# One cast and one subtraction per weight block of 2048 columns, in place of two of 1024 each

## The chip, the cores and the metric

The kernel runs on one core of one Trainium2 chip. What counts is the device time of one launch, in microseconds (us), as the median of several runs. The launch reads float32 inputs from device memory and writes a float32 output.

## What is computed

The reference is a two-layer trunk over 256 tokens of width 1024. Each layer is a half-step feed-forward block (FFN), a mixer (differential attention beside an mLSTM), and a second FFN, each between two RMS norms:

```python
def _swiglu(h, w_in, w_out):
    gate, up = jnp.split(h @ w_in, 2, axis=-1)          # w_in: 1024 x 5632
    return (jax.nn.silu(gate) * up) @ w_out             # w_out: 2816 x 1024

for l in range(DEPTH):                                   # DEPTH = 2
    g = norm_gains[l]
    h = _swiglu(_rmsnorm(x, g[0]), ffn_w_in[l, 0], ffn_w_out[l, 0])
    x = x + 0.5 * _rmsnorm(h, g[1])
    h = _mixer(_rmsnorm(x, g[2]), mix_w_in[l], mix_w_out[l], ...)
    x = x + _rmsnorm(h, g[3])
    h = _swiglu(_rmsnorm(x, g[4]), ffn_w_in[l, 1], ffn_w_out[l, 1])
    x = x + 0.5 * _rmsnorm(h, g[5])
```

Almost all of the arithmetic is the products with the weights, which are read once, in 164 blocks of 1 MB of float32.

## The kernel before

**Weights.** The weights come as *pieces* of 128 x 2048 float32 (1 MB), 33 to an FFN and 16 to a mixer. `fetch` (L283) loads a piece into a tile `wr`, or for every fourth piece of an FFN into a tile `wx`; there are three of the one and one of the other. A product in full precision is made of three matmuls on rounded operands, so every piece is taken apart into a rounded high part and a low part. `halved` (L291) does this for 1024 columns: ScalarE (ACT) casts them to the high tile `wh` (L295) and VectorE (DVE) subtracts that from the raw piece into the low tile `wl` (L296). A piece takes two such pairs of instructions. TensorE (PE) then does high x high, high x low and low x high (L506 to L508 in `mm3`; L762 in the pair steps; L737 and L742 at the end of an FFN).

**Buffers of the parts.** Seven tiles `wl` and seven tiles `wh` of 1024 columns rotate; three of every ten halves go to a third pool, `k4` (six of 1024 columns), which the mixer also uses for its own tiles through `t4`.

**An FFN.** The hidden units are taken in 11 chunks of 256. `STEPS` says what is loaded and done when: `I` are the two input pieces of a chunk, `L` an output piece, `O` the output matmuls of a chunk (`out_part`), `P` a *pair* of chunks whose first product is done with seven block products in place of eight. `pair_blocks` (L310) makes these seven operands: four raw pieces and the sums of some of them, which DVE adds in halves of 1024 columns (L322) into the tiles `qk` and `wt`, cast and subtracted like the pieces. The activations of a chunk go ACT, DVE, then through `planes` (an ACT copy), a transposing DMA and `hT` (another ACT copy) to the operands `hh` (ACT, L676) and `hl` (DVE, L677) of the output matmuls.

**The end of an FFN.** After the second pair step (`P8`) the last chunk is computed transposed by `in_turned` (L729), into four banks: two named `pin`, two named `ptr`. `ffn_block` (L689) evacuates each of these (ACT copies `su<-pin`, `su<-ptr`, L695; DVE L696 and L697). Directly behind `in_turned` on PE come the output matmuls of the pair's first chunk, whose operand is `hh<-hT` (L676); they are L506 to L508 on the banks `bk`. Meanwhile ACT has to do, for the pair: a SiLU `u<-u`, the copy `planes<-h`, and after its DMA `hT<-h` and `hh<-hT`; the same once more for the pair's second tokens (`planes<-v`, `hT<-v`).

**What sets the order.** A scheduler with its own estimate of times orders the instructions on each engine and decides what stands ahead of what; PE's order is written out only at the very end and the very start of an FFN or mixer (`manual_schedule`). Each engine then works through its own list strictly in order: an instruction that has to wait holds up all that stands behind it. The DMA lists on SyncE (SP) work in the same way.

**Exceptions.** In an FFN that follows a mixer or FFN, the first pieces' casts are tied to the norm before (`self.turns`), and are left in halves by the change as well; so are the mixer's pieces.

Of the kernel before, what the change touches and what calls it, by code (L numbers as in the profile page):

```python
# [17 lines left out]
F32 = mybir.dt.float32  # L18
F32R = mybir.dt.float32r
U16 = mybir.dt.uint16  # L20
AF = mybir.ActivationFunctionType
ALU = mybir.AluOpType
AX = mybir.AxisListType
PSUM = bass.MemoryType.PSUM

P = 128
D = 1024
S = 256
NT = S // P
# [106 lines left out]
class _Trunk:  # L136
    def __init__(self, tc, a, out, pools):
        self.tc, self.nc, self.a, self.out = tc, tc.nc, a, out
        self.const, self.wr, self.wl, self.wh, self.tr, self.k2, self.k4, self.ded, self.hp, self.sm, self.ps = pools
        self.piece_at = 0  # L140
        self.parts = None
        self.raws, self.four = 0, False
        self.n = 0
        self.turns = []
        self.halves = 0
        self.both = [None, None]
        self.lend = True

# [11 lines left out]
        return self.k2.tile(list(shape), dt, tag=tag, bufs=bufs, name=self.name(nm))  # L160

    def t4(self, nm, shape):
        return self.k4.tile(list(shape), F32, tag="k4", name=self.name(nm))

    def small(self, nm, shape, bufs=None):
        return self.sm.tile(list(shape), F32, tag=nm, name=self.name(nm))
# [105 lines left out]
    def piece(self):  # L272


        parts = self.begin_piece()
        return [parts(), parts()]

# [13 lines left out]
    def halved(self, raw):  # L291
# [8 lines left out]
            self.after(iv, [ov] if ov else [])  # L300
        return hi, lo

    def spare(self):
        if self.parts is None:
            self.qk = self.ded.tile([P, 4, S], F32, name="qk")
            self.wt = self.ded.tile([P, NT, 2, 2, P], F32, name="wt")
            self.parts = [self.qk.rearrange("p b s -> p (b s)"), self.wt.rearrange("p t a b j -> p (t a b j)")]
        return self.parts

    def pair_blocks(self):  # L310


        def fetch():
            raw = self.fetch()
            return [raw[:, j] for j in range(2)]

        def split(raw):
            return [self.halved(raw[j]) for j in range(2)]

        def add(out, a, b):  # L320
            for j in range(2):
                self.nc.vector.tensor_tensor(out[j], a[j], b[j], op=ALU.add)  # L322

        b11, b12 = fetch(), fetch()
        w = {"P1": split(b11)}
        run = self.spare()
        add(run, b11, b12)
        w["P5"] = split(run)
        b22 = fetch()
        add(run, run, b22)  # L330
        w["P6"] = split(run)
        add(b12, b12, b22)
        w["P7"] = split(b12)
        b21 = fetch()
        w["P2"] = split(b21)
        w["P3"] = split(b22)
        add(run, run, b21)
        w["P4"] = split(run)
        return w

    def pair_tokens(self, both, kept):
# [28 lines left out]
        def split(i):  # L370
            hi, lo = (tiles[i // 2][:, :, n + i % 2, :] for n in (0, NT))
            self.ffn_hilo(s, hi, lo)
            return hi, lo
# [9 lines left out]
        apart((0, 0), (0, 1))  # L383
        yield x1, x2, split(2), x4

    def half_tiles(self):

        pools = (self.k4, "k4", self.k4, "k4") if self.lend and self.halves % 10 in (2, 5, 8) else (self.wl, "wl", self.wh, "wh")
        self.halves += 1
        return [pools[n].tile([P, 1024], F32R, tag=pools[n + 1], name=self.name(nm)) for n, nm in ((0, "wl"), (2, "wh"))]  # L390

    def raw_tile(self, i):
        self.raws += 1
# [103 lines left out]
    @staticmethod  # L497
    def cols(piece, k):

        c = slice((k % 2) * 512, (k % 2) * 512 + 512)  # L500
        hi, lo = piece[k // 2]
        return hi[:, c], lo[:, c]
# [419 lines left out]

    def mixer(self, pre, gi_post):
        self.mixer_buffers()
        m = _Mixer(self, pre, gi_post // 3)
        ws = [self.piece(), self.piece()]
        self.lend = False
        ws1 = [self.piece()]
        pins, pins1 = [self.bank_pin()], [self.bank_pin()]
        m.part(0, 0, pins[0], ws[0])  # L930
        m.part(0, 1, pins[0], ws[1])
        m.gate_part(0)
        m.conv_input(0, pins[0])
        yield "second"
        m.part(0, 0, pins1[0], ws1[0])
        m.conv_input_t(0)
        pins.append(self.bank_pin())
        ws1.append(self.piece())
        m.gate_part(1)
        gpost = []  # L940
        m.traverse(self, pins[1], ws, pins1, ws1, lambda: gpost.append(self.load_gpost(gi_post)))
        gpost = gpost[0]


        self.lend = True
        ws = [self.piece() for _ in range(4)]
        po = [[self.bank_bk() for _ in range(2)] for _ in range(NT)]

        def outp(t, part, hf):
            for k in range(4):  # L950
                yh, yl = m.yT[t][part]
                self.mm3(po[t][hf], yh[:, k, :], yl[:, k, :], *self.cols(ws[2 * part + k // 2], 2 * (k % 2) + hf),
                         start=part == 0 and k == 0, stop=part == 1 and k == 3)

        outp(0, 0, 0)
        m.outputs_ml(0)
        outp(0, 0, 1)
        outp(0, 1, 0)
        m.outputs_ml(1)
        outp(0, 1, 1)  # L960
        yield "done", po[0], gpost
        outp(1, 0, 0)
        outp(1, 0, 1)
        yield "next"
        outp(1, 1, 0)
        outp(1, 1, 1)
        yield "done", po[1], gpost
# [472 lines left out]
def _trunk(tc, a, out, phases=3 * L):  # L1440
    nc = tc.nc
    with contextlib.ExitStack() as st:
        def pool(name, bufs, **kw):
            return st.enter_context(tc.tile_pool(name=name, bufs=bufs, **kw))

        fill = pool("fill", 1)
        fill.tile([P, FILL // 4], F32, name="fill")
        wr, wl, wh, trp, k4 = pool("wr", 3), pool("wl", 7), pool("wh", 7), pool("tr", 4), pool("k4", 6)
        hp, k2, const, ded = pool("hp", 4), pool("k2", 10), pool("const", 1), pool("ded", 1)
        const.tile([P, CFILL // 4], F32, name="cfill")  # L1450
        pools = (const, wr, wl, wh, trp, k2, k4, ded, hp, pool("sm", 2), pool("ps", 1, space=PSUM))
        tr = _Trunk(tc, a, out, pools)
        tr.x = [tr.const.tile([P, D], F32, name=f"x{t}") for t in range(NT)]
        tr.early = {}
        tr.start()
        tr.users = []
        tr.table("silu_and_others")
        tr.half = tr.const.tile([P, 16], F32, name="c_half")
        nc.gpsimd.memset(tr.half, -0.5)
        tr.run(phases)  # L1460
# [17 lines left out]
```

## Time and profile before

| | |
|---|---|
| median of 3 runs | 940.39 us (940.22 to 941.68) |
| the profiled execution | 940.3 us, span 938.5 us, granted TensorE clock 0.998 |
| PE busy | 931.4 us, 99% of the span, 4427 matmuls |
| DVE busy | 775.5 us, 83%, 1079 instructions |
| ACT busy | 668.4 us, 71%, 1033 instructions |
| DMA | 189.34 MB, 202 GB/s on average |

A row of a group reads: line, engine, operation, output<-inputs, partitions x elements, count, then total busy us and mean ns of one, then the idle time of the engine just before these instructions and what ended it. A row of a timeline reads: start in us from the start of the span, duration in us of the whole row (with x2, of both), engine, line, operation, and in brackets idle time before it and what released it. Rows that overlap by a tenth of a microsecond are normal: an engine starts the next instruction before the last one's end is written.

Where the work lies: FFN 1 of layer 0 runs from the start to about 175 us, the first mixer to about 300, then two FFNs to about 640, the second mixer to about 765, and the last FFN to the end. The ends of the four FFNs' `in_turned` are at 166, 453, 629 and 916 us.

### The profile page before, as it was taken

Reading aid. Unit: us, or ns where it says so; the run is one execution under the profiler, and the core shown is the slowest. Engines: PE = TensorE matmul, PEld = TensorE weight load, DVE = VectorE, ACT = ScalarE, POOL = GpSimd, SP = SyncE. Lnnn points to the kernel's source line nnn. Section 1 sums busy time; section 2 is a strip of 40 time slices with the busy share of each in tenths; the row PEclk is TensorE's granted clock in tenths of the full one; section 3 lists DMA queues with packets and bytes.
Section 4 is the critical chain, followed back from the end, with each engine's and each line's share of the span. In section 5 each row is a group of like instructions: output and inputs, shape, how many; then the busy total and the mean of one; then the engine's idle time right before and its main releaser. Section 6 shows DMA issues by size and latency. Waiting matters only on the chain.

```text
span 938.5 us, 12082 instructions
## 1 busy us (share of the span) xinstructions
PE 931.4 (99%) x4427; PEld 771.5 (82%) x4427; DVE 775.5 (83%) x1079; ACT 668.4 (71%) x1033; POOL 29.4 (3%) x57
## 2 busy tenths in 40 slices
PE   9999999999999999999999999999999999999997
PEld 7888888888888888888888888888888888888885
DVE  7989797889867899788698987968898588986974
ACT  8967786677856868676587865866778478766862
POOL 2000000000020000000000000000001100000000
PEclk9999999999999999999999999999999999999999
DMA  9957857346362866838468585473554348486531
GB/s 354 342 169 275 251 192 218 119 152 221 138 232 90 303 167 225 303 107 309 121 237 257 172 267 189 155 237 135 189 193 169 146 157 302 148 300 184 186 115 46
DMA packets 69882, 189.34 MB, mean 202 GB/s; under 512 B 45274, under 2 KB 46426, under 8 KB 49086
## 3 DMA queue, kind: packets, MB, share of 16 engines
q1 hardware_dynamic: 69246, 187.95, 59.1%
q8 instruction: 35, 0.57, 0.2%
q10 hardware_dynamic: 576, 0.61, 0.2%
q14 instruction: 25, 0.20, 0.1%
HBM read 177.01 MB, written 1.05 MB: 190 GB/s over the span
## 4 chain that ended last, share of the span: by engine, by line
PE 99%; DVE 0%; ACT 0%; POOLq 0%; DVEq 0%; issue 0%; ACTq 0%
PE pin L506 11%; PE pin L508 10%; PE pin L507 10%; PE bk L506 10%; PE bk L507 10%; PE bk L508 10%; PE ptr L762 9%; PE pin L762 7%; PE ptr L507 3%; PE ptr L506 3%; PE ptr L508 3%; PE ptr L737 2%; PE pin L737 2%; PE ptr L532 1%; PE ptr L1100 1%; PE pin L742 1%
## 5 line engine op out<-in xcount | busy, mean ns | idle before, releaser
L296 DVE TENSOR_TENSOR wl<-wr,wh 128x1024 fp32r<-128x1024 f32 x262 | 313.6, 1221 | 42.2 <-ACT wh L295 39.4
L295 ACT ACTIVATE wh<-wr 128x1024 fp32r<-128x1024 f32 x262 | 269.5, 1055 | 55.9 <-PE bk L508 15.8
L506 PE MATMUL pin<-wh,both 128*128 128x512 f32 x432 | 171.3, 399 | 0.0
L507 PE MATMUL pin<-wl,both 128*128 128x512 f32 x432 | 168.4, 390 | 0.0
L508 PE MATMUL pin<-wh,both 128*128 128x512 f32 x432 | 168.2, 390 | 0.0
L507 PE MATMUL bk<-wl,hh 128*128 128x512 f32 x352 | 136.3, 389 | 0.0
L506 PE MATMUL bk<-wh,hh 128*128 128x512 f32 x352 | 135.8, 390 | 0.0
L508 PE MATMUL bk<-wh,hl 128*128 128x512 f32 x352 | 133.4, 389 | 0.0
L508 PEld LDWEIGHTS pin<-wh,both 128*128 128x128 f32 x432 | 81.1, 188 | 17.4
L506 PEld LDWEIGHTS pin<-wh,both 128*128 128x128 f32 x432 | 81.3, 188 | 17.2 <-issue 0.7
L507 PEld LDWEIGHTS pin<-wl,both 128*128 128x128 f32 x432 | 81.3, 188 | 15.5
L295 ACT ACTIVATE wh<-wx 128x1024 fp32r<-128x1024 f32 x62 | 64.3, 1055 | 31.9 <-PE bk L508 10.2
L762 PE MATMUL ptr<-wh,both 128*128 128x512 f32 x256 | 84.0, 389 | 0.0
L296 DVE TENSOR_TENSOR wl<-wx,wh 128x1024 fp32r<-128x1024 f32 x62 | 74.7, 1220 | 10.2 <-ACT wh L295 9.5
L508 PEld LDWEIGHTS bk<-wh,hl 128*128 128x128 f32 x352 | 66.1, 188 | 13.8
L506 PEld LDWEIGHTS bk<-wh,hh 128*128 128x128 f32 x352 | 66.1, 188 | 13.5
L507 PEld LDWEIGHTS bk<-wl,hh 128*128 128x128 f32 x352 | 66.1, 188 | 13.4
L762 PE MATMUL pin<-wh,both 128*128 128x512 f32 x192 | 63.0, 389 | 0.0
L762 PEld LDWEIGHTS ptr<-wh,both 128*128 128x128 f32 x256 | 48.0, 188 | 10.0
L507 PE MATMUL ptr<-wl,both 128*128 128x512 f32 x128 | 49.8, 389 | 0.0
L508 PE MATMUL ptr<-wh,both 128*128 128x512 f32 x128 | 49.8, 389 | 0.0
L762 PE MATMUL ptr<-wl,both 128*128 128x512 f32 x128 | 49.8, 389 | 0.0
(263 smaller groups left out, 1464.2 us busy)
## 6 DMA issues: line engine op xcount, KB each, us to landing
wr<-in_w_dram SPq DMA_DIRECT2D x131, 1024.0 KB, 5.1
wx<-in_w_dram SPq DMA_DIRECT2D x31, 1024.0 KB, 5.0
gpost<-in_gpost_dram SPq DMA_DIRECT2D x6, 512.0 KB, 6.2
wr<-in_w_dram SPq DMA_DIRECT2D x2, 512.0 KB, 6.3
wr<-in_w_dram SPq DMA_DIRECT2D x3, 256.0 KB, 4.5
x<-in_x_dram SPq DMA_DIRECT2D x3, 256.0 KB, 5.2
h<-planes SPq DMA_TRANSPOSE x32, 3.3
out_dram<-x SPq DMA_DIRECT2D x2, 256.0 KB, 2.1
```

The lines of the kernel that those rows point to most:

```text
L295: ia = nc.scalar.activation(hi, raw, AF.Copy)
L296: iv = nc.vector.tensor_tensor(lo, raw, hi.bitcast(F32), op=ALU.subtract)
L506: mm(ps, xh, wh, start=start, stop=False)
L507: mm(ps, xh, wl, start=False, stop=False)
L508: mm(ps, xl, wh, start=False, stop=stop)
L532: nc.tensor.transpose(ptr[:, k, :], x[:, (4 * hf + k) * P:(4 * hf + k + 1) * P], self.ident)
L737: self.nc.tensor.matmul(b, self.cols(w[kh], k)[0][:, c], both[kh][:, k].rearrange("p i t -> p (i t)"), start=kh == 0 and k == 0, stop=Fals ...
L742: self.nc.tensor.matmul(b[:, 0:NT * P], self.cols(w[kh], k)[1][:, c], both[kh][:, k, 0:NT].rearrange("p i t -> p (i t)"), start=False, sto ...
L762: self.nc.tensor.matmul(b, st[:, k, :], self.cols(w, k)[mv], start=new and k == n == 0, stop=k == 3 and n == 2, skip_group_check=True)
L1100: self.T(ptr[:, b, :], a[:, b * P:(b + 1) * P], self.tr.ident)
```

## The change

`whole` casts and subtracts a piece of an FFN with one ACT and one DVE instruction of 2048 columns. The tiles for the parts become one pool `w` of seven tiles of 2 x 1024 columns for high and low together, with three more in `k4`; the bytes are the same as before. `halved` stays for mixer pieces and for the first pieces of an FFN, and takes the halves of one such tile. The sums of a pair lie side by side in one tile `sums`, and each is added, cast and subtracted by one instruction of 2048 columns. By count, ACT has 135 instructions fewer, DVE 167 (135 subtractions and 32 additions); PE, SP and POOL have as many as before.

```diff
     def piece(self):
+        if self.four and not self.turns:
+            return self.whole(self.fetch())
         parts = self.begin_piece()
         return [parts(), parts()]
...
+    def whole(self, raw):
+        lo, hi = self.piece_tiles()
+        self.cut = self.nc.scalar.activation(hi, raw, AF.Copy)
+        self.nc.vector.tensor_tensor(lo, raw, hi.bitcast(F32), op=ALU.subtract)
+        return [(hi[:, j], lo[:, j]) for j in range(2)]
...
     def pair_blocks(self):
-        def fetch():
-            raw = self.fetch()
-            return [raw[:, j] for j in range(2)]
-        def split(raw):
-            return [self.halved(raw[j]) for j in range(2)]
+        fetch, split = self.fetch, self.whole
         def add(out, a, b):
-            for j in range(2):
-                self.nc.vector.tensor_tensor(out[j], a[j], b[j], op=ALU.add)
+            self.nc.vector.tensor_tensor(out, a, b, op=ALU.add)
...
+    def piece_tiles(self):
+        v = []
+        for nm in ("wl", "wh"):
+            pool, tag = (self.k4, "k4") if self.lend and self.tiles % 10 in (2, 5, 8) else (self.w, "w")
+            v.append(pool.tile([P, 2, 1024], F32R, tag=tag, name=self.name(nm)))
+            self.tiles += 1
+        return v
...
-        wr, wl, wh, trp, k4 = pool("wr", 3), pool("wl", 7), pool("wh", 7), pool("tr", 4), pool("k4", 6)
+        wr, w, trp, k4 = pool("wr", 3), pool("w", 7), pool("tr", 4), pool("k4", 3)
```

Because fewer and longer instructions are scheduled, the lists of the engines change too. (In the changed kernel L295 is L304 for halves and L315 for whole pieces, L296 is L305 and L316, and the lines from L367 on are 11 to 23 higher: L648 is L671, L656 is L679, L676 is L699, L677 is L700, L695 is L718.)

The first place is DVE's list near the start of the launch. `aT` and `both` are the token operands of the first pair step, made there in several small steps. Before, `wr_305`, `wr_315` and `wx_395` are the fourth, fifth and sixth piece of the launch:

```order
L296 TENSOR_TENSOR wl_307<-wr_305,wh_308 128x1024
L296 TENSOR_TENSOR wl_311<-wr_305,wh_312 128x1024
L677 TENSOR_TENSOR both_495<-aT_90_497,both_495 128x4x128
L296 TENSOR_TENSOR wl_317<-wr_315,wh_318 128x1024
L367 TENSOR_TENSOR aT_90_497<-both_187,aT_90_497 128x512
L296 TENSOR_TENSOR wl_321<-wr_315,wh_322 128x1024
L296 TENSOR_TENSOR wl_397<-wx_395,wh_398 128x1024
L368 TENSOR_TENSOR aT_90_497<-aT_90_497,both_187 128x512
```

Now `wr_296`, `wr_302` and `wx_378` are the same three pieces:

```order
L316 TENSOR_TENSOR wl_298<-wr_296,wh_299 128x2048
L700 TENSOR_TENSOR both_466<-aT_74_468,both_466 128x4x128
L378 TENSOR_TENSOR aT_74_468<-both_182,aT_74_468 128x512
L316 TENSOR_TENSOR wl_304<-wr_302,wh_305 128x2048
L379 TENSOR_TENSOR aT_74_468<-aT_74_468,both_182 128x512
L316 TENSOR_TENSOR wl_380<-wx_378,wh_381 128x2048
```

The sixth piece's first half was subtracted ahead of the `aT` step of L368; now the whole sixth piece stands behind that step.

The second place is ACT's list at the end of the first FFN. Before, `wh_1655` is the second half of the FFN's last piece, and `hh_1523` the operand that the output matmuls directly behind `in_turned` need:

```order
L295 ACTIVATE wh_1655<-wr_1648 128x1024
L648 ACTIVATE planes_1404<-h_1314 128x1024
L686 ACTIVATE rows_1546<-ptr_1543 128x256
L648 ACTIVATE planes_1422<-v_1313 128x1024
L656 ACTIVATE hT_1531<-h_1314 128x2x512
L676 ACTIVATE hh_1523<-hT_1531 128x256
L695 ACTIVATE su_1622<-pin_1548 128x256
L676 ACTIVATE hh_1527<-hT_1531 128x256
L656 ACTIVATE hT_1537<-v_1313 128x2x512
L695 ACTIVATE su_1622<-pin_1549 128x256
```

Now `wh_1493` is the whole last piece, and `hh_1365` is that operand:

```order
L315 ACTIVATE wh_1493<-wr_1490 128x2048
L671 ACTIVATE planes_1266<-h_1176 128x1024
L709 ACTIVATE rows_1388<-ptr_1385 128x256
L718 ACTIVATE su_1464<-pin_1390 128x256
L671 ACTIVATE planes_1284<-v_1175 128x1024
L718 ACTIVATE su_1464<-pin_1391 128x256
L718 ACTIVATE su_1477<-ptr_1392 128x256
L274 ACTIVATE su_1464<-su_1464 128x256
L679 ACTIVATE hT_1373<-h_1176 128x2x512
L274 ACTIVATE su_1477<-su_1477 128x256
L718 ACTIVATE su_1477<-ptr_1393 128x256
L699 ACTIVATE hh_1365<-hT_1373 128x256
```

All four evacuations of `in_turned`, the last bank's `ptr_1393` among them, now stand ahead of `hh`; before, `hh` stood ahead of all four. At the end of the second FFN the same tail (`hT`, a SiLU, `su<-ptr` of the last bank, `hh`) has come about.

The third place is ACT's list at the end of the third FFN. Before, from the SiLU of the pair's second tokens on:

```order
L267 ACTIVATE u_5521<-u_5521,rs_922_4534 128x512
L648 ACTIVATE planes_5613<-h_5523 128x1024
L686 ACTIVATE rows_5755<-ptr_5752 128x256
L648 ACTIVATE planes_5631<-v_5522 128x1024
L656 ACTIVATE hT_5740<-h_5523 128x2x512
L676 ACTIVATE hh_5732<-hT_5740 128x256
L695 ACTIVATE su_5831<-pin_5757 128x256
```

Now:

```order
L718 ACTIVATE su_5335<-pin_5261 128x256
L274 ACTIVATE u_5045<-u_5045,rs_726_4180 128x512
L709 ACTIVATE rows_5259<-ptr_5256 128x256
L718 ACTIVATE su_5335<-pin_5262 128x256
L671 ACTIVATE planes_5137<-h_5047 128x1024
L718 ACTIVATE su_5348<-ptr_5263 128x256
L671 ACTIVATE planes_5155<-v_5046 128x1024
L274 ACTIVATE su_5335<-su_5335 128x256
L679 ACTIVATE hT_5244<-h_5047 128x2x512
L274 ACTIVATE su_5348<-su_5348 128x256
L718 ACTIVATE su_5348<-ptr_5264 128x256
L699 ACTIVATE hh_5236<-hT_5244 128x256
```

Here even `planes<-h`, which starts the way to `hh`, stands behind the evacuations of both `pin` banks. In the last FFN `planes<-h`, `hT` and `hh` still stand ahead of all four evacuations.

More of the change, by code (lines that the diff above doesn't have):

```diff
@@ L138, in __init__ @@
         self.tc, self.nc, self.a, self.out = tc, tc.nc, a, out
-        self.const, self.wr, self.wl, self.wh, self.tr, self.k2, self.k4, self.ded, self.hp, self.sm, self.ps = pools
+        self.const, self.wr, self.w, self.tr, self.k2, self.k4, self.ded, self.hp, self.sm, self.ps = pools
         self.piece_at = 0
@@ L144, in __init__ @@
         self.turns = []
-        self.halves = 0
+        self.tiles = 0
+        self.rest, self.lent = None, None
         self.both = [None, None]
@@ L162, in t4 @@
     def t4(self, nm, shape):
-        return self.k4.tile(list(shape), F32, tag="k4", name=self.name(nm))
+        if self.lent is None:
+            pair = self.k4.tile([P, 2, 1024], F32, tag="k4", name=self.name(nm))
+            v, self.lent = pair[:, 0], pair[:, 1]
+        else:
+            v, self.lent = self.lent, None
+        return v[0:shape[0]].rearrange("p (a b) -> p a b", a=shape[1])
     def small(self, nm, shape, bufs=None):
@@ L301, in halved @@
         return hi, lo
+    def whole(self, raw):
[3 more added lines that the diff above has]
+        return [(hi[:, j], lo[:, j]) for j in range(2)]
     def spare(self):
         if self.parts is None:
-            self.qk = self.ded.tile([P, 4, S], F32, name="qk")
-            self.wt = self.ded.tile([P, NT, 2, 2, P], F32, name="wt")
-            self.parts = [self.qk.rearrange("p b s -> p (b s)"), self.wt.rearrange("p t a b j -> p (t a b j)")]
+            self.sums = self.ded.tile([P, 2, 1024], F32, name="sums")
+            self.parts = [self.sums[:, j] for j in range(2)]
+            self.qk = self.parts[0].rearrange("p (b s) -> p b s", b=4)
+            self.wt = self.parts[1].rearrange("p (t a b j) -> p t a b j", t=NT, a=2, b=2)
         return self.parts
     def pair_blocks(self):
-        def fetch():
-            raw = self.fetch()
-            return [raw[:, j] for j in range(2)]
-        def split(raw):
-            return [self.halved(raw[j]) for j in range(2)]
+        fetch, split = self.fetch, self.whole
         def add(out, a, b):
-            for j in range(2):
-                self.nc.vector.tensor_tensor(out[j], a[j], b[j], op=ALU.add)
+            self.nc.vector.tensor_tensor(out, a, b, op=ALU.add)
         b11, b12 = fetch(), fetch()
         w = {"P1": split(b11)}
-        run = self.spare()
+        run = self.sums
         add(run, b11, b12)
@@ L384, in pair_tokens @@
         yield x1, x2, split(2), x4
-    def half_tiles(self):
-        pools = (self.k4, "k4", self.k4, "k4") if self.lend and self.halves % 10 in (2, 5, 8) else (self.wl, "wl", self.wh, "wh")
-        self.halves += 1
-        return [pools[n].tile([P, 1024], F32R, tag=pools[n + 1], name=self.name(nm)) for n, nm in ((0, "wl"), (2, "wh"))]
+    def piece_tiles(self):
[5 more added lines that the diff above has]
+        return v
+    def half_tiles(self):
+        if self.rest:
+            v, self.rest = self.rest, None
+            return v
+        tiles = self.piece_tiles()
+        self.rest = [v[:, 1] for v in tiles]
+        return [v[:, 0] for v in tiles]
     def raw_tile(self, i):
@@ L924, in mixer @@
         self.mixer_buffers()
+        self.lent = None
         m = _Mixer(self, pre, gi_post // 3)
@@ L1447, in _trunk @@
         fill.tile([P, FILL // 4], F32, name="fill")
-        wr, wl, wh, trp, k4 = pool("wr", 3), pool("wl", 7), pool("wh", 7), pool("tr", 4), pool("k4", 6)
+        wr, w, trp, k4 = pool("wr", 3), pool("w", 7), pool("tr", 4), pool("k4", 3)
         hp, k2, const, ded = pool("hp", 4), pool("k2", 10), pool("const", 1), pool("ded", 1)
         const.tile([P, CFILL // 4], F32, name="cfill")
-        pools = (const, wr, wl, wh, trp, k2, k4, ded, hp, pool("sm", 2), pool("ps", 1, space=PSUM))
+        pools = (const, wr, w, trp, k2, k4, ded, hp, pool("sm", 2), pool("ps", 1, space=PSUM))
         tr = _Trunk(tc, a, out, pools)
```

## Prediction

> **What bounds the kernel now.** I read the page first (engines, chain, groups), then the chain of waits piece by piece, then the timelines of PE, ACT and DVE at the places where a weight or an activation comes closest to the matmul that needs it.
>
> ```profile
> PE 931.4 (99%) x4427; PEld 771.5 (82%) x4427; DVE 775.5 (83%) x1079; ACT 668.4 (71%) x1033; POOL 29.4 (3%) x57
> PE 99%; DVE 0%; ACT 0%; POOLq 0%; DVEq 0%; issue 0%; ACTq 0%
> 351.65 2.72 PE ptr L762 x12
> ```
>
> The first line is engines' busy time, the second the chain that ended last, the third one of its pieces inside a pair step. PE is busy in 931.4 of 938.5 us and the chain is PE's own list: nobody makes it wait for long. Twelve matmuls of 512 columns take 2.72 us, 0.227 us each, and in the FFNs they follow one another like this without a hole. So at most 938.5 - 931.4 = 7.1 us of idle PE could be won anywhere, while every delay of a weight or an activation beyond its margin is lost time. What the change does to DVE's and ACT's busy time matters only through those margins.
>
> **What an instruction of 2048 columns costs.** The groups of the casts and subtractions, of two narrower and one similar shape, and two pairs in the timelines:
>
> ```profile
> L296 DVE TENSOR_TENSOR wl<-wr,wh 128x1024 fp32r<-128x1024 f32 x262 | 313.6, 1221 | 42.2 <-ACT wh L295 39.4
> L295 ACT ACTIVATE wh<-wr 128x1024 fp32r<-128x1024 f32 x262 | 269.5, 1055 | 55.9 <-PE bk L508 15.8
> L476 DVE TENSOR_TENSOR wl<-wr,wh 128x512 fp32r<-128x512 f32 x8 | 5.5, 685 | 0.6 <-ACT wh L472 0.5
> L472 ACT ACTIVATE wh<-wr 128x512 fp32r<-128x512 f32 x8 | 5.0, 636 | 0.7 <-DMA wr<-in_w_dram 0.6
> L322 DVE TENSOR_TENSOR wt<-wt,wr 128x1024 f32<-128x1024 f32 x14 | 17.1, 1219 | 0.0
> 22.26 2.35 DVE L296 TENSOR_TENSOR wl<-wr,wh 128x1024 fp32r<-128x1024 f32 x2
> 24.81 2.00 ACT L295 ACTIVATE wh<-wx 128x1024 fp32r<-128x1024 f32 x2
> ```
>
> No instruction of 2048 columns of this kind is in the trace; I extend the line through 512 and 1024. DVE: (1221 - 685)/512 = 1.047 ns a column and 149 ns fixed, so 2048 columns take 2.29 us, where two back to back take 2.35. The sums (1219 ns) behave alike. ACT: (1055 - 636)/512 = 0.818 ns a column and 217 ns fixed, so 1.89 us, where two take 2.00. A merged pair therefore saves about 0.06 us of DVE and 0.10 us of ACT. The bounds are nothing saved (2.35 and 2.00, if the line bends) and the fixed parts whole (0.15 and 0.22). Over the launch that is 167 x 0.06 = 10 us of DVE and 135 x 0.10 = 14 us of ACT, all of it beside PE, which the second line above says nobody holds up: worth nothing by itself.
>
> What is lost is earliness. The first half of a high part is ready 1.89 - 1.05 = 0.84 us later. Its low part starts only after the whole cast and ends after 2.29 in place of 1.22: 1.9 us later if DVE waits for the cast. The Trainium skill has a rule on this, in "Perfetto Trace Analysis", section Optimizing Scalar/DVE Operations: larger operations help an engine that is saturated, and where Scalar and Vector aren't, but cause bubbles on other engines, breaking them up may finish work sooner. With ACT at 71% and DVE at 83% it speaks against merging, and its 60 ns (DVE) and 93 ns (Scalar) of overhead per instruction would make the savings 167 x 0.06 = 10.0 and 135 x 0.093 = 12.6 us, an estimate by that page that agrees with the rows above.
>
> **Term 1: the start.** DVE and PE in the first 31 us:
>
> ```profile
> 24.53 0.68 DVE L677 TENSOR_TENSOR both<-aT,both 128x512 fp32r<-128x512 f32 x1
> 25.13 1.22 DVE L296 TENSOR_TENSOR wl<-wr,wh 128x1024 fp32r<-128x1024 f32 x1
> 26.27 0.69 DVE L367 TENSOR_TENSOR aT<-both,aT 128x512 f32<-128x512 f32 x1
> 28.01 1.22 DVE L296 TENSOR_TENSOR wl<-wx,wh 128x1024 fp32r<-128x1024 f32 x1
> 29.14 0.69 DVE L368 TENSOR_TENSOR aT<-aT,both 128x512 f32<-128x512 f32 x1
> 24.56 0.39 PE L507 MATMUL pin<-wl,both 128*128 128x512 f32 x1
> 30.00 0.39 PE L507 MATMUL ptr<-wl,both 128*128 128x512 f32 x1
> ```
>
> DVE runs here without a pause. The sixth piece's first low half is done at 28.01 + 1.22 = 29.23, and PE wants it at 30.00. By the new list: the fourth piece's whole subtraction from 22.26 to 24.55 (PE wants it at 24.56: it just fits, at worst 0.1 late), the next starts 0.08 before an end, as in these rows (25.13 + 1.22 against 26.27), so `both` at 24.47, `aT` at 25.07, the fifth piece at 25.67, the second `aT` step, now ahead, at 27.88, the sixth piece from 28.48 to 30.77. PE then stands 0.8 us behind the two matmuls on the high part that it can do before. Bounds 0 and 1.0; I take **0.8**. It replaces no wait, and the casts on ACT for these pieces run earlier (24.81) and cover themselves.
>
> **Term 2: the ends of the first three FFNs.** The rows of before, three FFNs and the fourth in a row:
>
> ```profile
> 156.72 1.04 ACT L648 ACTIVATE planes<-h 128x1024 uint16<-128x1024 uint16 x1
> 161.12 1.37 ACT L656 ACTIVATE hT<-h 128x1024 uint16<-128x1024 uint16 x1 [2.14 <-DMA h<-planes]
> 162.52 0.42 ACT L676 ACTIVATE hh<-hT 128x256 fp32r<-128x256 f32 x1
> 166.03 0.40 PE L506 MATMUL bk<-wh,hh 128*128 128x512 f32 x1
> 443.30 1.04 ACT L648 ACTIVATE planes<-h 128x1024 uint16<-128x1024 uint16 x1
> 448.81 1.37 ACT L656 ACTIVATE hT<-h 128x1024 uint16<-128x1024 uint16 x1 [0.27 <-DMA h<-planes]
> 452.35 0.38 ACT L695 ACTIVATE su<-ptr 128x256 f32<-128x256 f32 x1 [0.83 <-PE ptr L742]
> 452.63 0.40 PE L506 MATMUL bk<-wh,hh 128*128 128x512 f32 x1
> 619.72 1.04 ACT L648 ACTIVATE planes<-h 128x1024 uint16<-128x1024 uint16 x1
> 623.93 1.37 ACT L656 ACTIVATE hT<-h 128x1024 uint16<-128x1024 uint16 x1 [0.67 <-DMA h<-planes]
> 629.05 0.40 PE L506 MATMUL bk<-wh,hh 128*128 128x512 f32 x1
> 915.40 0.86 ACT L695 ACTIVATE su<-ptr 128x256 f32<-128x256 f32 x2
> 915.68 0.40 PE L506 MATMUL bk<-wh,hh 128*128 128x512 f32 x1
> ```
>
> Before, `hh` is ready some 3 us early (162.94 against 166.03). Now it stands on ACT's list behind `su<-ptr` of the last bank, and that copy has to wait for the last matmul of `in_turned`, directly behind which PE wants `hh`. Nothing else stands on PE's list there, so this can't be hidden. Its price from these rows: in the fourth FFN the second of the two `su<-ptr` ends at 915.40 + 0.86 = 916.26 and so starts at about 915.9, 0.22 after PE could have gone on (915.68); then 0.38 less the overlap of 0.1, then `hh` 0.42 and some 0.05 until PE starts: 0.22 + 0.28 + 0.42 + 0.05 = 0.97, say **0.95** in each of three FFNs, whenever the data came.
>
> On top of it the data come later. First FFN: the whole cast of the last piece but one now waits for a tile that PE gives free at about 154.7 (counted along PE's list), the SiLU `u` comes at 157.0, the last piece's whole cast follows (1.89), and `planes<-h` ends at 160.45 in place of 157.76. With the way to `hT` of before (161.12 - 157.76 = 3.36 us) `hT` is ready by 165.2, under the copy at 166.25: the term stays at 0.95. Second FFN: the same queue makes `planes<-h` end at 447.0; its way took 448.81 - 444.34 = 4.47 us, so `hT` starts at 451.5; each next ACT instruction starts 0.1 before the end of the last, so the SiLU comes at 452.75, the copy at 453.05, `hh` from 453.33 to 453.75, against 452.63: **1.2**. Third FFN: `planes<-h` stands behind both `pin` copies. The two `ptr` banks are now computed whole behind the `pin` banks, each as long as twelve matmuls of 512 (2.72), so the `pin` banks are complete at 629.05 - 5.44 = 623.6, the first slightly before. ACT: copy 623.1, `u` 623.4, rows 624.0, copy 624.3, `planes<-h` 624.6 to 625.65; the way took 623.93 - 620.76 = 3.17, so `hT` from 628.8, SiLU 630.05, copy 630.35, `hh` done 631.0, against 629.05: **2.0**. Bounds of the three together: 2.85 (the queue alone) and, with 4.47 us for the way in all three, 1.2 + 1.2 + 3.3 = 5.7. In the fourth FFN `hh` keeps its place ahead of the copies: 0.
>
> **Nothing for the rest.** In the pair steps the high and low parts and the sums come later, but their margins are mostly 3 to 6 us. The tightest operand there is in the first pair:
>
> ```profile
> 79.45 0.71 ACT L676 ACTIVATE hh<-hT 128x256 fp32r<-128x256 f32 x2
> 81.23 0.62 PE L506 MATMUL bk<-wh,hh 128*128 128x512 f32 x2
> ```
>
> It is ready at 80.16 with 1.07 to spare; followed through the new list it is done at 80.4, 0.8 ahead. The mixers keep their halves, and PE's list in them is the same but for names; ACT's and DVE's differ in a few places. I put 0 there, with 0.5 to either side each.
>
> **The sum.** 0.8 + 0.95 + 1.2 + 2.0 = 4.95 us. The durations are those of the profiled execution, 940.3 us with a span of 938.5; the median of the runs is 940.39, the same. 940.3 + 4.95 = **945.3 us**, 0.5% slower. Its own range: 940.3 + 2.85 = 943.2 (no loss at the start) to 940.3 + 1.0 + 5.7 + 1.0 = 948.
>
> **Rivals.**
>
> *Only the start is lost.* If the copies out of `ptr` did not wait for the last matmul, or PE could do other work there, the ends would cost nothing: 940.3 + 0.8 = 941.1. For it: 3 us of margin in each end before. Against it: the row at 452.35 names PE's `ptr` as what it waited for, and the 0.86 us of the two copies at 915.40 are stretched by the same wait. Chance 0.13.
>
> *The pair steps stall as well.* Each FFN has two, whose operands form a chain of sum, cast and subtraction. If the margins I counted are 1 us too optimistic, the first half of a sum, 1.9 us later than now, makes PE wait in each of eight: at 0.5 to 1.0 apiece, 945.3 + 4 to 8, about 951. It decides where a margin is below 1.9; the row at 79.45 has one of 1.07. Against it: that operand isn't in the chain, and weights in the pairs have more. Chance 0.12.
>
> *Faster.* If DVE and ACT, not PE, are what the 7.1 us of idle PE wait for, above all in the mixers, 10 us less DVE and 14 us less ACT work shorten some of them. For it: DVE's idle time is by far mostly for ACT's casts (39.4 of 42.2). Against it: the chain gives 0% to both, and the merged instructions are mostly not in the mixers. A third of the 7.1 us would be 2.4: 937.9. The Trainium skill's "VectorE: DVE Perf Modes", section Rules for kernel authors, asks to minimize the count of chained DVE operations, since each is followed by a drain; by that rule this is what should happen. The rows show it as the 0.06 us per pair, which agrees, but off the path. It decides if the ends lose less than 2.4. Chance 0.09.
>
> **How the numbers follow.** The forecast has 0.66 and gives 945.3. About 0.2% (1.9 us) is what a measurement of this kernel can tell from no change. Faster: the third rival but for a part that the losses eat, 0.07. Same: the first rival and that part, 0.16. Slower: the forecast and the second, 0.77. The range goes from 941.0, to take in the first rival, to 949.0, a little beyond the forecast's own end: 0.63 of the forecast, the first rival and the mildest part of the second make 0.8.
>
> **What would show it.** Right: a merged subtraction near 2.29 us and a cast near 1.89; a hole on PE of 0.8 us at about 30 us, released by DVE's `wl`; holes of 0.9 to 2 us at the first output matmul behind `in_turned` near 167, 454 and 632, released by ACT's `hh`, none near 920; PE's pace in pairs unchanged. Wrong: no hole there, holes behind L785 in pair steps, a different length of the mixers, or merged instructions much longer than 2.35 and 2.00.

## The result and the profile after

The changed kernel takes 954.42 us in the median (952.79 to 956.4) against 940.31 (939.9 to 941.68) for the kernel before: ratio 1.0148, interval 1.0124 to 1.0173. It is 1.5% slower. The forecast was 945.3, with a range of 941 to 949: the direction was right, the loss about three times as large. The profiled execution took 955.41 us, with a span of 953.5.

From the page of the changed kernel, first the engines and the chain that ended last, then the groups of the merged instructions and of the first output matmul, then the DMA issues:

```profile
PE 935.7 (98%) x4427; PEld 772.7 (81%) x4427; DVE 763.2 (80%) x912; ACT 649.2 (68%) x898; POOL 31.2 (3%) x57
PE 92%; DVE 3%; DMA 2%; ACT 2%; issue 1%; SPq 0%; POOLq 0%; DVEq 0%; ACTq 0%
L316 DVE TENSOR_TENSOR wl<-wr,wh 128x2048 fp32r<-128x2048 f32 x83 | 188.6, 2287 | 25.7 <-issue 8.8
L315 ACT ACTIVATE wh<-wr 128x2048 fp32r<-128x2048 f32 x83 | 156.5, 1908 | 27.4 <-PE ptr L785 10.9
L529 PE MATMUL bk<-wh,hh 128*128 128x512 f32 x352 | 135.2, 395 | 7.3 <-ACT hh L699 7.3
h<-planes SPq DMA_TRANSPOSE x32, 4.4
```

The saving is there: DVE is busy 12.3 us less (775.5 to 763.2), ACT 19.2 us less (668.4 to 649.2). It buys nothing, because PE holds the end. PE now waits 7.3 us for `hh` alone, and the chain, which was PE's by 99%, is 92% PE's, with DVE, DMA and ACT in the rest. The transposing DMAs take 4.4 us from issue to landing in the median; the same row of the page before reads 3.3.

PE's timeline of the changed kernel, at every place outside the first 25 us where it waits over half a microsecond:

```profile
31.40 0.50 PE L530 MATMUL ptr<-wl,both 128*128 128x512 f32 x1 [0.56 <-DVE wl L316]
170.94 0.71 PE L529 MATMUL bk<-wh,hh 128*128 128x512 f32 x1 [3.18 <-ACT hh L699]
222.41 0.50 PE L1243 MATMUL bk<-md,ul 100*128 100x512 f32 x1 [2.00 <-DVE md L1233]
463.97 0.50 PE L529 MATMUL bk<-wh,hh 128*128 128x512 f32 x1 [2.45 <-ACT hh L699]
644.13 0.50 PE L529 MATMUL bk<-wh,hh 128*128 128x512 f32 x1 [1.64 <-ACT hh L699]
```

A *hole* below is the distance between the starts of two neighbouring matmuls, less the 0.227 us that a matmul of 512 columns takes (for a shorter one, what it takes elsewhere); it is 0.16 longer than the idle time in the brackets, since the first matmul after a wait takes longer to get going. The five are holes of 0.72, 3.34, 2.16, 2.62 and 1.81 us. They make 10.7 of the 15.0 us between the two profiled executions (953.5 less 938.5). Where the rest lies, PE's rows grouped by stretch show. The columns are the stretch, its length, busy time and count of PE, PEld, DVE, ACT and POOL, then the granted clock, the DMA share and GB/s:

```profile
171.00:174.40 3.40, 3.40 (x8) 2.67 (x9) 2.14 (x7) 2.17 (x4) 0.00 (x0) 0.51 0.30 128
464.50:468.10 3.60, 3.60 (x10) 2.84 (x10) 1.67 (x5) 1.69 (x3) 0.00 (x0) 0.53 0.17 71
644.10:648.00 3.90, 3.87 (x17) 3.11 (x18) 1.47 (x5) 1.56 (x2) 0.00 (x0) 1.00 0.51 118
```

Behind the holes of 3.34 and 2.62 us PE has half its clock for 3.4 to 3.6 us: 8 and 10 matmuls, where a full clock gives 15 and 16 (3.40 and 3.60 by 0.227). Behind that of 1.81 it has not.

Both executions have 4427 matmuls on PE's list. The start of the n-th matmul in the changed one, less the start of the n-th in the one before, grows from place to place as follows:

| place | forecast | measured | of it half clock |
|---|---|---|---|
| first 25 us | 0 | 0.65 | |
| sixth piece, 30 us | 0.8 | 0.9 | |
| end of FFN 1 | 0.95 | 5.05 | 1.7 |
| first mixer | 0 | 2.15 | |
| end of FFN 2 | 1.2 | 4.3 | 1.7 |
| end of FFN 3 | 2.0 | 1.95 | |
| end of FFN 4, pair steps, elsewhere | 0 | 0.0 | |
| sum | 4.95 | 15.0 | 3.4 |

### The profile page after: what moved, and what is told of

Read it like the earlier page. It is cut to its first block, busy times and chain, and to the rows that moved or that the text cites. A ratio compares the mean times of both kernels' runs of the same rounds, so it can differ in the third digit from the quotient of the medians.

```text
span 953.5 us, 11708 instructions
## 1 busy us (share of the span) xinstructions
PE 935.7 (98%) x4427; PEld 772.7 (81%) x4427; DVE 763.2 (80%) x912; ACT 649.2 (68%) x898; POOL 31.2 (3%) x57
## 4 chain that ended last, share of the span: by engine, by line
PE 92%; DVE 3%; DMA 2%; ACT 2%; issue 1%; SPq 0%; POOLq 0%; DVEq 0%; ACTq 0%
PE bk L529 10%; PE bk L531 10%; PE bk L530 10%; PE pin L529 10%; PE pin L531 10%; PE pin L530 10%; PE ptr L785 9%; PE pin L785 7%; PE ptr L530 3%; PE ptr L531 3%; PE ptr L529 3%; DMA h<-planes 2%; PE ptr L555 1%; PE pin L760 1%; PE ptr L1124 1%; ACT wh L315 1%
## 5 line engine op out<-in xcount | busy, mean ns | idle before, releaser
L316 DVE TENSOR_TENSOR wl<-wr,wh 128x2048 fp32r<-128x2048 f32 x83 | 188.6, 2287 | 25.7 <-issue 8.8
L315 ACT ACTIVATE wh<-wr 128x2048 fp32r<-128x2048 f32 x83 | 156.5, 1908 | 27.4 <-PE ptr L785 10.9
L305 DVE TENSOR_TENSOR wl<-wr,wh 128x1024 fp32r<-128x1024 f32 x96 | 113.8, 1221 | 13.5 <-ACT wh L304 11.6
L304 ACT ACTIVATE wh<-wr 128x1024 fp32r<-128x1024 f32 x96 | 96.3, 1050 | 14.2 <-PE bk L531 3.3
L785 PE MATMUL ptr<-wh,both 128*128 128x512 f32 x256 | 83.7, 389 | 0.0
L316 DVE TENSOR_TENSOR wl<-wx,wh 128x2048 fp32r<-128x2048 f32 x28 | 64.1, 2289 | 22.4 <-ACT wh L315 10.3
L315 ACT ACTIVATE wh<-wx 128x2048 fp32r<-128x2048 f32 x28 | 53.5, 1911 | 40.9 <-PE ptr L785 21.3
L315 ACT ACTIVATE wh<-sums 128x2048 fp32r<-128x2048 f32 x24 | 45.9, 1914 | 49.6 <-PE pin L785 13.9
L316 DVE TENSOR_TENSOR wl<-sums,wh 128x2048 fp32r<-128x2048 f32 x24 | 54.9, 2288 | 21.5 <-ACT wh L315 21.5
```

The source lines that it names most:

```text
L304: ia = nc.scalar.activation(hi, raw, AF.Copy)
L305: iv = nc.vector.tensor_tensor(lo, raw, hi.bitcast(F32), op=ALU.subtract)
L315: self.cut = self.nc.scalar.activation(hi, raw, AF.Copy)
L316: self.nc.vector.tensor_tensor(lo, raw, hi.bitcast(F32), op=ALU.subtract)
L785: self.nc.tensor.matmul(b, st[:, k, :], self.cols(w, k)[mv], start=new and k == n == 0, stop=k == 3 and n == 2, skip_group_check=True)
```

## Why the data are late at the end of FFN 1

From the lists of SP (DMA issues), DVE and ACT at the end of FFN 1, in the kernel before, then in the changed one:

```profile
142.31 11.53 SPq L288 DMA_DIRECT2D wr<-in_w_dram  x4
157.79 1.27 SPq L650 DMA_TRANSPOSE h<-planes  x1
...
152.27 1.22 DVE L296 TENSOR_TENSOR wl<-wr,wh 128x1024 fp32r<-128x1024 f32 x1
```

```profile
150.72 10.79 SPq L297 DMA_DIRECT2D wr<-in_w_dram  x3
161.95 1.34 SPq L673 DMA_TRANSPOSE h<-planes  x1
...
158.87 2.29 DVE L316 TENSOR_TENSOR wl<-wr,wh 128x2048 fp32r<-128x2048 f32 x1
...
156.65 1.92 ACT L315 ACTIVATE wh<-wr 128x2048 fp32r<-128x2048 f32 x1 [5.79 <-PE ptr L785]
159.08 1.90 ACT L315 ACTIVATE wh<-wr 128x2048 fp32r<-128x2048 f32 x1
160.89 1.04 ACT L671 ACTIVATE planes<-h 128x1024 uint16<-128x1024 uint16 x1
168.71 1.34 ACT L679 ACTIVATE hT<-h 128x1024 uint16<-128x1024 uint16 x1 [3.03 <-DMA h<-planes]
170.48 0.71 ACT L699 ACTIVATE hh<-hT 128x256 fp32r<-128x256 f32 x2
```

Before, the last weight load ahead of the transposes was issued by 153.84, 3.95 us ahead of them. Now the last of three is issued by 161.51, 0.44 us ahead, and lands 6.3 us after its issue began, so that 1 MB is under way when `h<-planes` starts. From the end of `planes<-h` to `hT` it now takes 168.71 - 161.93 = 6.78 us, where it took 3.36. The row at 156.65 says why the load is late: the cast of the last piece but one waits 5.79 us for a tile that PE frees whole. The load has to wait for the raw tile that this piece's subtraction frees: the subtraction ends at 158.87 + 2.29 = 161.16, the load is issued at 161.18, and the profile puts SP's wait down to DVE's L316. Before, the subtraction of the same piece's second half ended at 153.49, and the load was issued at 153.51. e2 tests the load, e4 the length of the instructions.

## The experiments

All but the last two are compared with the kernel before by several runs of each; its median in these comparisons was 940.6 to 940.7.

**The order on ACT's list alone (e1).** All four evacuations of `in_turned` are made to stand behind the first two `hh`, which `ahead` holds.

```diff
+            self.after(nc.scalar.activation(su[:, i], bank[i][:, n:2 * n], AF.Copy), self.ahead)
```

> The changed kernel with one thing added: at the end of each FFN the four evacuations of in_turned must stand behind the first two hh on ACT's list, as the kernel before had it. Theory A (late data): at the ends of FFN 1 and 2 the loss is there because the transposing DMA takes 6.8 and 6.1 us behind a weight load, hT starts at 168.7 and 461.7 whatever stands on ACT's list, so the holes shrink only by the 0.6 us of the SiLU and the copy, from 3.3 and 2.6 to 2.7 and 2.0; at the end of FFN 3, where planes<-h moves forward by 4 us, the hole of 1.8 goes. About 951. Theory B (the queue alone): all three holes go, and the slow matmuls behind them with them: 954.4 - 3.3 - 2.6 - 1.8 - 3.3 = 943.

953.87 us (953.13 to 955.71), ratio 1.0145 (1.0131 to 1.0159). ACT and PE with `hh` ahead of the copies:

```profile
168.71 1.34 ACT L680 ACTIVATE hT<-h 128x1024 uint16<-128x1024 uint16 x1 [5.81 <-DMA h<-planes]
170.09 0.72 ACT L700 ACTIVATE hh<-hT 128x256 fp32r<-128x256 f32 x2
...
170.56 0.80 PE L530 MATMUL bk<-wh,hh 128*128 128x512 f32 x1 [3.03 <-ACT hh L700]
463.38 0.50 PE L530 MATMUL bk<-wh,hh 128*128 128x512 f32 x1 [2.12 <-ACT hh L700]
642.67 0.50 PE L530 MATMUL bk<-wh,hh 128*128 128x512 f32 x1 [0.71 <-ACT hh L700]
```

`hT` starts at 168.71, as it did in the changed kernel: nothing is won by a place on the list for data that aren't there. At the ends of FFN 1 and 2 the order is worth 0.15 and 0.3 us; only at the end of FFN 3, where the data come in time, is it about 0.9. The queue, on which the forecast was built, isn't what makes the two large holes. The time of neither theory came: at the end of FFN 3 a hole stays, and behind the other two the half clock does.

**The loads behind the transposes (e2).** Two loads, those issued just ahead of the transposes at the ends of FFN 1 and 2, are put behind these on SP's list.

```diff
         self.load = nc.sync.dma_start(raw.rearrange("p a b -> p (a b)"), self.a["w"][i])
+        if i in (34, 85):
+            self.after(self.load, self.turned[-2:])
```

> The changed kernel, but one weight load each at the ends of FFN 1 and 2 (the one issued just ahead of the transposes) is put behind them on SP's list. The scheduler, which now expects the data sooner, also puts hh ahead of the last su<-ptr there by itself; the end of FFN 3 has its list as in the changed kernel. Theory A: the transposes land within 3.2 to 3.6 us, the holes at 167 and 461 fall from 3.3 and 2.6 to below 0.4, the slow matmuls behind them go, FFN 3 keeps its 1.8: 954.4 - 2.9 - 2.2 - 3.3 = 946. Rival (the transposes are slow for a reason of their own): 6 us to landing as now, holes of 2.7 and 2.0: 953.

947.77 us (946.36 to 948.63), ratio 1.0075 (1.0061 to 1.0089): 6.65 us below the changed kernel. With the loads out of the way:

```profile
159.93 1.04 ACT L674 ACTIVATE planes<-h 128x1024 uint16<-128x1024 uint16 x1
164.65 1.37 ACT L682 ACTIVATE hT<-h 128x1024 uint16<-128x1024 uint16 x1 [1.63 <-DMA h<-planes]
```

The way is 164.65 - 160.97 = 3.68 us, and 3.27 at the end of FFN 2. No hole over 0.3 us is left at these two ends, no half clock follows there, and those of FFN 3 (idle 1.68) and the mixer (1.99) stay. So the loads are the cause of both large ends, the half clock included. `hh` also stands ahead of the last `su<-ptr` again, though nothing was said of it; e1 shows that this is worth 0.15 and 0.3 at most. The Trainium skill, "DMA: Bandwidth & Descriptors", section Issuing engines are not separate DMA queues, says that DMAs, whichever engine issued them, run on the same 16 DMA engines and interleave with each other; 6.78 against 3.68 us, with and without a weight load ahead, agrees.

**PE kept at work during the wait (e3).** At these two ends 13 and 10 matmuls by zeros stand in the hole; they add nothing to the result.

```diff
+        for _ in range({0: 13, 2: 10}.get(gi_post, 0)):
+            i = self.nc.tensor.matmul(po[1][1], zero.broadcast_to([P, P]), zero.broadcast_to([P, 512]), start=False, stop=False, ...)
+            self.after(i, self.lastmm)
```

> The changed kernel with 13 and 10 matmuls of zeros (added into an output bank, so that it stays as it is) between in_turned and the first output matmul of FFN 1 and 2, where PE waits 3.3 and 2.6 us; ACT's list there is unchanged. Theory C (the waiting itself makes PE slow afterwards: twelve matmuls per 4.4 to 5.1 us in place of 2.7): the output matmuls that follow go at 0.227 us from the first on, 1.6 us won at each end, 951. Rival (they are slow because of their operands, or the data): spacing 0.43 as now, 954.4 or a little more.

951.69 us (951.06 to 952.26), ratio 1.0119 (1.0105 to 1.0133), 2.7 below the changed kernel. The stretches behind the two ends, to be read beside the clock rows above:

```profile
171.20:174.40 3.20, 3.20 (x15) 2.55 (x14) 2.20 (x8) 2.41 (x5) 0.00 (x0) 1.00 0.23 95
462.60:466.00 3.40, 3.40 (x16) 2.73 (x15) 2.37 (x8) 2.44 (x5) 0.00 (x0) 1.00 0.20 84
```

`hh` comes no earlier, yet the clock stays full. The mean granted clock is 0.998 in all four timed executions, as in the kernel before; in those of the changed kernel it is 0.994 to 0.998. The half clock follows from PE's idling, and is a second price on the same wait.

**Halves in the wide tiles (e4).** Everything is cast, subtracted and added in 1024 columns again, while the pools and the double-width tiles of the change stay.

```diff
         lo, hi = self.piece_tiles()
...
+            for j in range(2):
+                self.cut = self.nc.scalar.activation(hi[:, j], raw[:, j], AF.Copy)
+                self.nc.vector.tensor_tensor(lo[:, j], raw[:, j], hi[:, j].bitcast(F32), op=ALU.subtract)
...
         def add(out, a, b):
-            self.nc.vector.tensor_tensor(out, a, b, op=ALU.add)
+            for j in range(2):
+                self.nc.vector.tensor_tensor(out[:, j], a[:, j], b[:, j], op=ALU.add)
```

> The changed kernel's double-width tiles and pools, but every cast, subtraction and addition in halves of 1024 columns again. Theory L (the length of the instructions is what moves the lists and delays the data): no hole at 30 us, no or small holes at the ends of the FFNs, 941 to 943. Rival W (the double-width tiles, which come free only when both halves are used, are what delays): holes at the ends like those of the changed kernel, 950 or more, though the one at 30 us goes.

944.17 us (943.57 to 945.8), ratio 1.0041 (1.0028 to 1.0054). The length of the instructions thus costs 10.25 of the 14.1 us: the start and the ends. What stays is the first mixer:

```profile
216.51 0.80 PE L1249 MATMUL bk<-md,ul 100*128 100x512 f32 x1 [1.99 <-DVE md L1239]
```

Half clock follows this wait in the profiled execution. The mixer's own instructions were halves all along, so the tiles must be what costs there; e5 tests it.

**A tile of its own for each half (e5).** The merged instructions stay; a half of the mixer (and of an FFN's first pieces) takes one wide tile for its own high and low part, in place of half of two tiles which it shares with the next half.

```diff
     def half_tiles(self):
-        if self.rest:
-            v, self.rest = self.rest, None
-            return v
-        tiles = self.piece_tiles()
-        self.rest = [v[:, 1] for v in tiles]
-        return [v[:, 0] for v in tiles]
+        ...
+        v = pool.tile([P, 2, 1024], F32R, tag=tag, name=self.name("wlh"))
+        return [v[:, 0], v[:, 1]]
```

> The changed kernel, but where a piece stays in halves (mixers, first pieces of an FFN) a double-width tile holds the high and the low part of one half, in place of one part of both halves: a tile comes free as soon as that half is used, as before. Theory G (in the mixer the wide tiles come free too late): the hole of 2.2 us at 220 us, in the first mixer, goes. Its rival (the mixer suffers from the order of something else): the hole stays. A side effect that tests the account of the FFN ends: the scheduler now gives the end of the fourth FFN the list of the third (planes<-h behind both pin copies, hh behind the last su<-ptr), which had no hole so far and by that account gets one of about 1.8. Theory G with it: 954.4 - 2.2 + 1.8 = 954; rival 956.

951.83 us (951.21 to 952.3), ratio 1.0118 (1.0104 to 1.0132). DVE's list in the first mixer, of the kernel before, of the changed one, and of this one:

```profile
210.17 2.36 DVE L296 TENSOR_TENSOR wl<-wr,wh 128x1024 fp32r<-128x1024 f32 x2
212.56 1.29 DVE L1209 SCALAR_TENSOR_TENSOR md<-mh,c_hot 36x512 fp32r<-36x512 f32 x2
```

```profile
218.00 2.36 DVE L305 TENSOR_TENSOR wl<-wr,wh 128x1024 fp32r<-128x1024 f32 x2
220.28 0.68 DVE L1303 TENSOR_TENSOR ra<-rv,c 128x512 f32<-128x512 f32 x1
220.88 0.75 DVE L1308 TENSOR_TENSOR rb<-rv,c 128x256 f32<-128x256 f32 x2
221.67 1.29 DVE L1233 SCALAR_TENSOR_TENSOR md<-mh,c_hot 36x512 fp32r<-36x512 f32 x2
```

```profile
214.24 2.36 DVE L305 TENSOR_TENSOR wlh<-wr,wlh 128x1024 fp32r<-128x1024 f32 x2
216.63 1.29 DVE L1231 SCALAR_TENSOR_TENSOR md<-mh,c_hot 36x512 fp32r<-36x512 f32 x2
...
926.46 0.50 PE L527 MATMUL bk<-wh,hh 128*128 128x512 f32 x1 [1.63 <-ACT hh L697]
```

With shared tiles `md` came behind `ra` and `rb` (1.4 us) and behind a pair of subtractions that starts later; with tiles of their own the old order is back and the mixer's hole is gone. So the shared tiles cost it; that the scheduler moves `md` because they come free in pairs is argued, not shown. The last row is a new hole, of 1.79 us, at the end of FFN 4, where the other lists now put `hh` late. At the ends of FFN 1 and 2 there are holes of 3.32 and 2.87 us as in the changed kernel, but in the profiled execution no half clock behind them; the median is 2 us below the 954 that was expected.

**The start in halves (e8).** Only the launch's first seven pieces are taken in halves.

```diff
+        if self.piece_at <= 7:
+            for j in range(2): ...
```

> The changed kernel with the fourth to sixth piece of the launch in halves. By term 1 of the prediction the hole of 0.7 us at 30 us goes, and nothing else: 953.5. If PE only meets the next late operand there: a hole of like size soon after, 954.4.

952.91 us (951.92 to 954.48), ratio 1.0131 (1.0117 to 1.0145). The hole at 30 us is gone and no other has come in its place; the rest stay.

**Everything mended, with the whole pieces kept (e6).** The edits of e1, e2 and e5, and halves for the first pieces.

> The changed kernel with all causes found so far undone, whole pieces and sums otherwise kept: tiles of their own for halves, pieces four to six of the launch in halves, the weight load behind the transposes at the ends of FFN 1 and 2, hh ahead of the evacuations at all ends. If the account is complete: no hole at 30 us, none in the mixer, 0.3 at the first two ends, 0.9 and 0.4 as in E1 at the third and likewise at the fourth, 940.7 + 0.6 + 2.6 = 944. If a cause is missing (the pair steps, for instance): 947 or more.

942.59 us (942.2 to 943.4), ratio 1.0021 (1.0012 to 1.003).

```profile
PE 932.2 (99%) x4427; PEld 770.9 (82%) x4427; DVE 763.6 (81%) x917; ACT 649.2 (69%) x903; POOL 33.1 (4%) x57
PE 96%; DMA 1%; issue 1%; ACT 1%; DVE 1%; POOLq 0%; DVEq 0%; ACTq 0%
629.92 0.50 PE L531 MATMUL bk<-wh,hh 128*128 128x512 f32 x1 [0.72 <-ACT hh L701]
917.85 0.50 PE L531 MATMUL bk<-wh,hh 128*128 128x512 f32 x1 [0.67 <-ACT hh L701]
```

11.8 of the 14.1 us are back, and of what is left, about 2.0, the two holes of 0.89 and 0.84 us make 1.7. DVE and ACT have the saving still, and even without these two holes the kernel would be no faster than before: 942.59 - 1.73 = 940.9, an estimate from these rows, against 940.62. No version run here beats the kernel before.

**Whole instructions in the pair steps alone (e7).** Pieces in halves with tiles as in e5; only a pair's operands and sums stay whole.

```diff
     def piece(self):
-        if self.four and not self.turns:
-            return self.whole(self.fetch())
         parts = self.begin_piece()
```

> Whole casts, subtractions and additions in the pair steps alone (64 of the merged pairs, and the 32 sums); every other piece in halves with tiles of their own. If whole pieces hurt only where a single piece is waited for (the start, the ends), the pair steps cost nothing: 941 to 942. If they delay the pair steps, whose first product needs the first half early: holes behind L785 and 944 or more.

951.1 us (949.25 to 953.82), ratio 1.0114 (1.0096 to 1.0132), some 10 us above what was expected.

```profile
81.99 0.50 PE L781 MATMUL ptr<-wl,both 128*128 128x512 f32 x1 [0.79 <-DVE wl L314]
460.67 0.80 PE L525 MATMUL bk<-wlh,hh 128*128 128x512 f32 x1 [3.58 <-ACT hh L695]
...
449.14 0.34 SPq L295 DMA_DIRECT2D wx<-in_w_dram  x1
450.24 1.25 SPq L669 DMA_TRANSPOSE h<-planes  x1
```

This is a different list, with a load again right ahead of the transposes at the end of FFN 2 and the largest hole of all (3.74 us) behind it. The pair steps have four holes of 0.5 to 0.95 us here, 2.4 in all and released by whole subtractions, where the changed kernel has none. So that the pair steps cost nothing held for the list of the changed kernel and not for this one; why, no run shows. Most of the loss is the collision at the end of FFN 2 and the half clock behind it, which shows how easily it comes about.

**The changed kernel twice more (e9, e10).** Unaltered, for the clock.

> The changed kernel once more, unaltered, for its clock alone. Theory A: half the clock after a wait of PE is a property of the execution, not of the wait's length; then in this execution the stretches 171.0 to 174.4 and 464.5 to 468.1 us may show a granted clock of 1.00 where the first profile had 0.51 and 0.53, while the holes at 167.5 and 461.2 stay at 3.3 and 2.6 us; the span is then about 2 us shorter for each stretch at full clock. Theory B: a wait above some length always halves it; then both stretches show about 0.5 again and the span is 953 to 954 us.

> As the run before it, a third profile of the same kernel. By theory A its two stretches need not agree with either of the others; by theory B both show about 0.5.

One time each, 958.47 and 958.14 us, with 942.42 for the kernel before on the same chip. Below are rows by stretch, with the columns as above and the stretches cut on a grid of 3.41 us that is explained behind them. The first is of the changed kernel's first profile, in the mixer; then come the mixer and the end of FFN 1 of its second profile (e9), and last the end of FFN 1 of e5:

```profile
218.85:222.26 3.41, 1.56 (x8) 0.95 (x6) 3.38 (x6) 2.88 (x6) 0.00 (x0) 1.00 0.93 389
```

```profile
221.70:225.11 3.41, 1.41 (x6) 0.75 (x5) 3.31 (x8) 2.00 (x5) 0.00 (x0) 1.00 0.80 320
225.11:228.52 3.41, 3.41 (x10) 2.67 (x9) 3.41 (x8) 2.57 (x4) 0.00 (x0) 0.50 0.50 197
170.50:173.91 3.41, 2.73 (x7) 2.16 (x8) 2.51 (x7) 2.91 (x7) 0.00 (x0) 0.50 0.56 235
173.91:177.32 3.41, 3.41 (x9) 2.65 (x8) 0.51 (x3) 0.51 (x2) 0.00 (x0) 0.50 0.01 2
```

```profile
165.03:168.44 3.41, 1.78 (x12) 1.41 (x10) 0.52 (x2) 0.69 (x1) 0.00 (x0) 1.00 1.33 185
168.44:171.86 3.42, 1.89 (x8) 1.49 (x9) 1.76 (x5) 3.39 (x8) 0.00 (x0) 1.00 0.64 268
```

Neither theory as written holds. Both ends are slow in all three profiles of this kernel, which the first did not require; but the mixer's wait of 2.00 us, harmless in the first profile, is followed by half clock in the other two, and the half clock behind FFN 1 lasts 3.4 us in one and 6.8 in the others, which the second excludes.

The traces fit a third reading. Within an execution the half clock starts only on a grid of 3.41 us, and it lasts one step of it or two: in the first profile it starts at 171.06 and 464.60, 86 steps apart, in e9 at 170.50, 225.11 and 467.45, 16 and 71 steps apart. Taken step by step over all twelve profiles from 25 us on, every step at full clock in which PE is busy for 1.43 us or less is followed by one at half clock (the shortest wait that did this is 2.0 us), and no step with over 1.5 is. In the rows above, the mixer's wait leaves PE 1.56 us in one execution and 1.41 in the other, and e5's wait of 3.16 us is harmless because it is split over two steps, with 1.78 and 1.89. So the same wait costs half clock or not by how it falls on the grid, and the grid lies elsewhere in each execution.

## Why the prediction was wrong

**What held.** The merged subtraction takes 2.287 us (forecast 2.29) and the cast 1.908 (1.89). The start: 0.72 us of hole (0.8), and e8 takes it away. The end of FFN 3: 1.81 (2.0), with 3.18 us from `planes<-h` (done at 638.72) to `hT` (641.90), where 3.17 was assumed. FFN 4 and the pair steps: nothing. The savings on DVE and ACT are worth nothing even where all else is mended (e6), so the third rival is refuted. So is the first: the ends cost most. The second rival, stalls in the pair steps, did not occur in this kernel, though it did in e7. The two large holes lie where the forecast had holes and are released by `hh`, as its signs said; that is luck, since the reason given was another one. The rule of the Trainium skill's "Perfetto Trace Analysis", section Optimizing Scalar/DVE Operations, that breaking up instructions which cause bubbles on other engines may let the work be done sooner, was the right one of the two cited: in halves again (e4) the kernel is 10.25 us faster.

**The step that failed first: "with the way to `hT` of before".** The forecast moved `planes<-h` rightly: to 160.45, and it came at 161.93, with PE's list 1.56 us late by then. But it kept the DMA's time behind it, 3.36 us, with 4.47 as the upper bound. It followed PE's, ACT's and DVE's lists, and not SP's: it did not ask which weight load a later tile lets loose, and where that load then falls. Measured 6.78 and, at the end of FFN 2, `planes<-h` done at 455.68 and `hT` at 461.74, 6.06. This accounts for 3.34 and 2.62 us of hole, where the forecast had 0.95 and 1.2; e1 shows that the cause named for these, the place of `hh` behind `su<-ptr`, is worth 0.15 and 0.3 there.

**A price that was not in the sum.** Half clock behind the two waits: 1.7 us each in the profiled execution. Without it e3 wins 2.7; without the holes as well e2 wins 6.65.

**"The mixers keep their halves": 0.** They keep them in tiles that are shared and come free in pairs. Measured 2.16 us of hole in the first mixer, in e4 with no merged instruction at all, and none in e5. The forecast looked at PE's list there, which is the same, and put nothing for those of ACT and DVE, which "differ in a few places".

The 0.65 us in the first 25 belong to no step: PE's 101st matmul starts at 23.88 us in the execution before, at 24.52 in the changed one, and anywhere from 23.46 to 24.66 in the profiles of the experiments.

## What to carry to other kernels

An instruction or tile made twice as large holds its buffer until the second half is used, so everything that waits for that buffer comes later, loads included: follow SP's list to the transfer that is urgent, and look for what now runs beside it. Price a wait of the busiest engine by more than its length where its clock may drop; here one of 2 us or more cost 1.7 us or more on top in some executions and nothing in others. Busy time saved on engines that aren't the bound is worth what the chain of waits says, here nothing.

## What the hardware showed

*Transposes beside a load.* A transposing DMA issued 0.44 us behind a 1 MB weight load brought its data 6.78 us after `planes<-h`, against 3.36 and 3.68 us with no load close ahead. In the seven profiles with a load 0.43 to 0.45 us ahead of it at the ends of FFN 1 and 2 this way took 5.6 to 7.1 us each time; at the ends of the FFNs where the last load was issued over 5 us ahead, it took 3.1 to 4.3.

*The clock.* In these profiles the granted clock was decided step by step on a grid of 3.41 us: half in the step behind one in which PE was busy for 1.43 us or less, full behind one with over 1.5. Behind a step at half clock the next was at half again where PE had been busy for 2.35 to 2.73 us of it (three times), and full where it had been for 3.3 or more. So a wait of 2.0 us or more may bring half clock for 3.4 or 6.8 us. At the end of FFN 1, with 3.0 to 3.3 us idle, it did in the three profiles of the changed kernel and in e1, and not in e5 (3.16) and e8 (3.15). At the end of FFN 2, with 2.0 to 2.5 us idle, it did in those four and in e8; with 3.58 us it did in e7, with 2.71 it did not in e5. Behind the mixer's 2.0 us it did in e2, e4, e9 and e10, and not in the first profile, e1, e3 and e8. No wait of 1.7 us or less did. The Trainium skill's "TensorE: Matmul & The Clock Gate", section What's actually happening, gives half clock as the state after at least one idle window of about 3.4 us and says that the window runs freely, without regard to the kernel. The grid of 3.41 us agrees with such a window; that the window has to be idle does not, since up to 1.43 us of work in it were not enough to keep the clock. Where exactly between 1.43 and 1.5 us the limit lies, and whether it is the same for matmuls of other kinds, no run here shows.
